# A gated two-branch encoder block: the last two gate tiles of branch B as a pair of seven block products, two more warming products, another seed for near ties

## The chip, the cores and the metric

One core of one Trainium2 chip. The time is device microseconds of one execution of the kernel; the kernel before was run three times (424.71, 424.83 and 425.92 us, median 424.83), and one more execution was profiled.

## The reference

The input is x of 512 tokens by 1024 channels. It is normalised, and one projection gives everything: latents for a dense attention (branch A), queries, keys and values for a sparse attention (branch B), an indexer, a silu gate for each branch, and two sigmoid gates.

```
h = rmsnorm(x, norm_g)
q_lat, c_kv, k_rope, z_a, q_b, k_b, v_b, z_b, q_idx, k_idx, w_idx, gate_a, gate_b = split(h @ w_in)
y_a = mla_attention(...) * silu(z_a)
y_b = dsa_attention(...) * silu(z_b)
merged = sigmoid(gate_a) * (y_a @ w_o_a) + sigmoid(gate_b) * (y_b @ w_o_b)
out = rmsnorm(x + merged @ w_out, final_g)
```

Each gate is 512 tokens by 1024 channels, each silu path 512 by 512.

## The kernel before

The whole program is one function, `tile_block`. It describes the work as some dozens of generators ("threads"), each of which yields steps: an engine, an estimated time, the tiles written and read, and a function that emits the instructions. A planner (`Flow.run`, L192) keeps estimated free times of PE, DVE, ACT, POOL and SP, and emits the step that can start soonest by its estimate. To that start it adds 0.01 times the thread's priority and a `nudge`, a random number below 0.01 us that each thread draws when it is spawned (L154) from a generator seeded with `DRAW` (L151, L258). So the order on every engine is fixed when the program is built, and `DRAW` settles only steps that nearly tie. A step may name two engines (DVE or POOL); the planner takes the one that would end first.

**Precision.** Every fp32 operand of a product is split into a high part (ACT casts it, L314) and a low part (a subtraction on DVE or POOL, L340 or L342), and a product is three matmuls: high by high, high by low, low by high (`mm3`, L417; all matmuls are emitted by `mm`, L407, whose matmul is on L412).

**Projections.** They are computed in tiles of 128 channels by 512 tokens, with the 1024 input channels in 8 blocks. A single tile (`proj`, L959) is 8 x 3 matmuls of 512 columns; its weights come as one load into one of 4 raw buffers and are split in two halves of 512 columns (2 casts, 2 low parts). A pair of tiles (`proj2`, L1009) treats its two weight tiles as four blocks, and the normalised input as four blocks of its own (`input_sums`, L981, whose sums `hs` are already there), and computes the pair by seven block products in place of eight: `prep` makes four sums of weight blocks on DVE or POOL and splits seven blocks; each block product is 4 x 3 matmuls of 256 columns (`times`, L1046); `seven` (L1071) gathers the results with two ACT copies and five DVE sums of 256 columns, while it chains the products on three banks: a bank is added to again only when it has been read. Parts of pairs take at most 10 slots (`PCAP`), parts of other tiles at most 8 (`WCAP`).

**The order of the tiles** is written out in `QUEUE` (L2042). Lower-case names are single tiles and upper-case ones pairs: `ga` and `gb` are the gates of A and B, `za` and `zb` the silu paths, `sb` a key and a query tile of branch B, `VB` its values, and `ou` one preparation of output weights (load, split), which has no product of its own. Loads (`fetcher`, L928), splits (`splitter`, L938) and products (`multiplier`, L951) each go through the list in its order; the preparations of pairs and of output weights run beside the splitter as threads of their own. The products are filling work with low priority between the attention heads, the last of which run from about 300 to 326 us.

**What waits for the tiles.** `y_gate` (L1654) multiplies a branch's attention output by its silu path and, after all pairs are done ("pairs", L1109), splits it for the next product (`s_ys`, the split on L323 and L351). After the last projection of any kind ("projections", L1216) the gates of A, which were sent to DRAM, are loaded back (`fetch_gates`, L1250: eight loads `s_sig<-bias_scratch`). Then `branch_out` (L1713) computes eight tiles of branch A and eight of branch B, each 4 x 3 matmuls of 512 columns on `s_ys,s_w` with weights `w_o`, then the final product with the output weights (`s_wo`), residual and norm.

**The start.** `warm_up` (L517) issues `NWARM` = 14 bf16 matmuls of 256 columns on zeros (L522) while the first loads run; `early_mm` (L686) then has the first products.

Of the kernel before, what the change touches and what calls it, by code (L numbers as in the profile page):

```python
# [19 lines left out]
P = 128  # L20
# [23 lines left out]
class Buf:  # L44


    def __init__(self, tile, name):
        self.tile, self.name, self.w, self.r, self.written = tile, name, 0.0, 0.0, False
        self.by, self.reads = None, {}
# [31 lines left out]
class Step:  # L81
# [7 lines left out]

    def __init__(self, options, outs, ins):  # L90
        self.options, self.outs, self.ins = options, outs, ins


class Get:
# [28 lines left out]
def put(*bufs):  # L123
    for b in bufs:
        b.home.used[b.cls] -= 1
        b.home.free.append(b)
# [7 lines left out]
class Flow:  # L134
# [9 lines left out]
    def __init__(self):  # L144
# [5 lines left out]

        self.draw = random.Random(DRAW)  # L151

# [102 lines left out]
RAW_LAG = {"DVE": 0.125, "POOL": 0.1, "ACT": 0.1}  # L255
BIAS = 0.01
NUDGE = 0.01
DRAW = 53  # L258
PSQUARE = -50
SETTLE = {'PE': {'DVE': 2.0, 'ACT': 2.0, 'POOL': 2.0, 'SP': 1.0}, 'SP': {'DVE': 1.0, 'ACT': 1.0, 'POOL': 1.0}}  # L260
TC_ARGS = {}
# [3 lines left out]
def tile_block(ctx: ExitStack, tc: tile.TileContext, a: dict, out: bass.AP, bias_dram: bass.AP):  # L265
    nc = tc.nc
# [6 lines left out]
    def fixed(name, shape, dt=F32):  # L273
        return Buf(const.tile(shape, dt, name=name), name)
# [24 lines left out]
    def bank(cls):  # L299
        return Get(PS, cls, {"mm": 3, "lg": 2, "pt": 2, "pv": 1, "e": 6}.get(cls))  # L300
# [5 lines left out]
    def bufs(*vs):  # L306
        return [v.buf for v in vs if isinstance(v, View)]
# [94 lines left out]
    def pe(time, outs, ins, emit, count=1):  # L402
        step = Step([("PE", time, emit)], bufs(*outs), bufs(*ins))
        step.count = count
        return step
# [81 lines left out]
    zeros = fixed("zeros", [P, P])  # L487
# [29 lines left out]
    def warm_up():  # L517

        ps = yield bank("pv")
        z = zeros.tile.bitcast(BF16)  # L520
        for _ in range(NWARM):
            yield pe(WARM, [ps.all], [zeros.all], lambda: nc.tensor.matmul(  # L522
                ps.tile[:, :256], z[:, :P], z, start=True, stop=True))
        put(ps)

    def setup_pool():
# [1439 lines left out]
    outs = [(p, c) for p, n in ((1, 2), (7, 4), (2, 2), (6, 2), (5, 4), (4, 2), (3, 2)) for c in range(n)]  # L1966
    for item in QUEUE.split():
        kind, n = item[:2].lower(), item[2:]
# [24 lines left out]
    spawn(setup(), 0)  # L1993
    spawn(loads(), 0)
    spawn(warm_up(), 0)
    spawn(setup_pool(), PSET)
    spawn(early_x(), 0)
# [31 lines left out]
NWARM = 14  # L2029
WARM = 0.22  # L2030
# [8 lines left out]
PHEAD = 4.0  # L2039
OUT_AT = (0, 2, 4, 8, 10, 11, 13)  # L2040
ORDER = [0,1,2,3]
QUEUE = 'ga0 ga1 pe ma0 va0 ga2 za0 ma1 va1 ga3 za1 ma2 ga4 za2 ma3 ga5 za3 sb0 zb0 ga6 ga7 sb1 VB GB0 GB1 sb2 zb1 GB2 GB3 sb3 zb2 GB4 GB5 ou zb3 gb6 ou gb7 ou'  # L2042
LATE = 0.5
SLOW = 1.36
PSUMS = 8.0
# [85 lines left out]
```

## Time and profile before

| | us |
|---|---|
| three runs, median (lowest to highest) | 424.83 (424.71 to 425.92) |
| profiled execution, its own time | 424.27 |
| its span, first to last instruction | 422.5 |
| PE busy | 414.6 |
| DVE busy | 372.9 |
| ACT busy | 265.3 |
| POOL busy | 124.3 |

The profiled execution lasts 1.8 us longer than its span. An engine's busy time is the union of its instructions' times. A matmul is shown with its latency (about 0.39 us for 512 columns), so neighbours overlap, and how long one holds PE is read from start to start. In a timeline, instructions of one kind are merged into one row with their count; the brackets at its end say how long the engine was idle before it and what released it.

### The profile page before, as it was taken

The numbers are of one execution on the slowest core, as the hardware profiler recorded it, in microseconds if no ns is written. First come the engines' busy times: TensorE is split into PE (matmuls) and PEld (weight loads), VectorE is DVE, ScalarE is ACT, GpSimd is POOL, SyncE is SP. The second block draws the span as 40 slices with busy tenths as digits, with TensorE's granted clock in tenths as the row PEclk, the third lists the DMA queues.
The fourth block names the chain that finished last, engine by engine and source line by source line (L and its number), as shares of the span: only waits on it lengthen the run. The fifth ranks groups of instructions, "written<-read, shape, count | busy, mean of one in ns | idle before, by whom it ended". The sixth has DMA issues, their size and how long they took to land.

```text
span 422.5 us, 7070 instructions
## 1 busy us (share of the span) xinstructions
PE 414.6 (98%) x2312; PEld 364.4 (86%) x2312; DVE 372.9 (88%) x797; ACT 265.3 (63%) x596; POOL 124.3 (29%) x139
## 2 busy tenths in 40 slices
PE   8999999999999999999999999999999999999994
PEld 7999878788888888888999988998998888888883
DVE  5689889569999999999999999979799768999985
ACT  6787778576763748635568777694598434336624
POOL 0037768534464659500013000210100000110652
PEclk9999999999999999999999999999999999999998
DMA  7983136746256351454552346245541887248305
GB/s 261 384 303 102 48 97 187 225 119 158 76 154 177 89 158 50 114 150 149 144 169 75 109 142 162 79 149 141 143 151 61 278 310 250 98 145 285 146 1 199
DMA packets 30645, 65.89 MB, mean 156 GB/s; under 512 B 4776, under 2 KB 6200, under 8 KB 30608
## 3 DMA queue, kind: packets, MB, share of 16 engines
q1 hardware_dynamic: 28256, 61.66, 46.3%
q10 hardware_dynamic: 1584, 2.62, 1.7%
q0 software_dynamic: 768, 1.15, 0.9%
q8 instruction: 18, 0.29, 0.3%
q14 instruction: 19, 0.16, 0.1%
HBM read 50.49 MB, written 4.21 MB: 129 GB/s over the span
## 4 chain that ended last, share of the span: by engine, by line
PE 77%; DVE 7%; DMA 6%; ACT 4%; issue 2%; SPq 2%; POOL 0%; POOLq 0%; DVEq 0%; ACTq 0%
PE ps L412 69%; PE ps L429 4%; DMA s_x<-xT 3%; SPq L439 2%; DVE s_tmp L351 2%; DVE s_tmp L340 2%; DMA s_xn<-x 1%; PE ps L1547 1%; PE ps L1548 1%; PE ps L1546 1%; ACT ps L323 1%; DMA raw<-w_ql 1%; DMA s_op<-kpel 1%; ACT junk L323 1%; DVE s_h L340 1%
## 5 line engine op out<-in xcount | busy, mean ns | idle before, releaser
L412 PE MATMUL ps<-s_h,s_w 128*128 128x512 f32 (+1 forms) x732 | 169.9, 379 | 0.0
L412 PEld LDWEIGHTS ps<-s_h,s_w 128*128 128x128 f32 x732 | 128.3, 189 | 22.0
L314 ACT CAST s_w<-raw 128x512 fp32r<-128x512 f32 (+3 forms) x124 | 71.8, 593 | 18.2 <-DMA raw<-w_o 8.4
L342 POOL TENSOR_TENSOR s_w<-raw,s_w 128x512 fp32r<-128x512 f32 (+2 forms) x39 | 48.5, 1253 | 47.6 <-ACT s_w L314 43.7
L340 DVE TENSOR_TENSOR s_w<-raw,s_w 128x512 fp32r<-128x512 f32 (+2 forms) x85 | 55.9, 670 | 4.4 <-ACT s_w L314 3.9
L412 PE MATMUL ps<-s_ys,s_w 128*128 128x512 f32 x192 | 43.8, 389 | 0.0
L412 PEld LDWEIGHTS ps<-s_ys,s_w 128*128 128x128 f32 x192 | 36.0, 188 | 7.5
L323 ACT ACTIVATE s_p<-s_p,sm 128x128 f32<-128x128 f32 (+3 forms) x62 | 32.8, 552 | 4.9 <-DVE sm L1626 4.3
L412 PE MATMUL ps<-s_wo,s_mg 128*128 128x512 f32 (+1 forms) x156 | 33.2, 373 | 0.0
L412 PE MATMUL ps<-s_w,s_xg 128*128 128x328 f32 (+1 forms) x192 | 32.5, 323 | 0.0
L412 PEld LDWEIGHTS ps<-s_wo,s_mg 128*128 128x128 f32 x156 | 27.6, 188 | 5.2
L412 PEld LDWEIGHTS ps<-s_w,s_xg 128*128 128x128 f32 x192 | 31.4, 188 | 0.0
L340 DVE TENSOR_TENSOR s_ph<-ps,s_ph 128x384 fp32r<-128x384 f32 (+1 forms) x48 | 27.6, 592 | 0.7 <-ACT s_ph L314 0.5
L314 ACT CAST s_ph<-ps 128x384 fp32r<-128x384 f32 (+1 forms) x48 | 23.4, 516 | 6.4 <-PE ps L429 5.0
L323 ACT ACTIVATE s_p<-ps,sm 128x128 f32<-128x128 f32 (+3 forms) x32 | 16.8, 528 | 16.7 <-DVE sm L1529 16.6
L342 POOL TENSOR_TENSOR s_p<-s_bias,mask 128x128 f32<-128x128 f32 (+2 forms) x5 | 4.4, 890 | 75.5 <-DMA s_bias<-bias_scratch 75.5
L880 DVE MAX8 sm<-mask 128x8 f32<-128x384 f32 (+2 forms) x48 | 25.7, 548 | 0.2
L881 DVE MATCH_REPLACE8 mask<-sm,mask 128x384 f32<-128x384 f32 (+2 forms) x48 | 25.8, 540 | 0.0
L412 PE MATMUL ps<-s_ph,vv 128*128 128x512 f32 (+3 forms) x128 | 25.1, 318 | 0.0
L429 PE MATMUL ps<-ident,s_p 128*128 128x128 f32 x160 | 23.1, 273 | 0.0
L412 PEld LDWEIGHTS ps<-s_ph,vv 128*128 128x128 f32 x128 | 21.0, 188 | 2.4
L1529 DVE TENSOR_REDUCE sm<-ps 128x1 f32<-128x128 f32 (+3 forms) x32 | 14.8, 480 | 8.2 <-PE ps L1548 7.8
(194 smaller groups left out, 767.6 us busy)
## 6 DMA issues: line engine op xcount, KB each, us to landing
raw<-w_out SPq DMA_DIRECT2D x18, 512.0 KB, 4.8
s_op<-s_op SPq DMA_DIRECT2D x36, 128.0 KB, 2.7
raw<-w_ga SPq DMA_DIRECT2D x8, 512.0 KB, 3.7
raw<-w_gb SPq DMA_DIRECT2D x8, 512.0 KB, 3.6
raw<-w_o SPq DMA_DIRECT2D x16, 256.0 KB, 3.4
s_xn<-x SPq DMA_DIRECT2D x8, 256.0 KB, 5.1
bias_scratch<-s_sig ACTq DMA_DIRECT2D x8, 256.0 KB, 3.7
raw<-w_za SPq DMA_DIRECT2D x4, 512.0 KB
```

What stands on the lines that cost most here:

```text
L314: nc.scalar.copy(dst.ap, src.ap)
L323: nc.scalar.activation(dst.ap, src.ap, func, **kw)
L340: opts.append(("DVE", 0.07 + 0.00104 * x.n, lambda: nc.vector.tensor_tensor(dst.ap, x.ap, y.ap, op=op)))
L342: opts.append(("POOL", 0.15 + 0.0021 * x.n, lambda: nc.gpsimd.tensor_tensor(dst.ap, x.ap, y.ap, op=op)))
L351: lambda: nc.vector.scalar_tensor_tensor(dst.ap, x.ap, sc(s), y.ap, op0=op0, op1=op1))],
L412: nc.tensor.matmul(ps.ap, l.ap, r.ap, start=start and i == 0, stop=stop and i == len(pairs) - 1, skip_group_check=more)
L429: nc.tensor.transpose(d.ap, s.ap, ident.tile)
L439: return Step([("SP", n / 360000.0, lambda: nc.sync.dma_start(d, s))], bufs(dst), bufs(src))
L880: yield Step([("DVE", t, lambda: nc.vector.max(m8.tile, work.tile))], [m8], [work])
L881: yield Step([("DVE", t, lambda: nc.vector.match_replace(work.tile, m8.tile, work.tile, MARK))], [work], [m8])
L1529: yield Step([("DVE", 0.07 + 0.00104 * n, lambda: nc.vector.tensor_reduce(mx.tile[:, 1:2], ps.tile[:, :n], op=ALU.max, axis=AX.X, negate=T ...
L1546: nc.tensor.matmul(o, q0[0:100], k0[0:100], start=True, stop=False)
```

## The change

Gate tiles 6 and 7 of branch B, two single tiles near the end of the list, become a pair directly behind the pair of tiles 4 and 5. The single silu tile `zb3` moves behind it, and of the three preparations of output weights that stood between these tiles, one stays ahead of `zb3` and two come behind it. The last warming step emits three matmuls in place of one, 16 in all, at the same planned time. The seed of the nudges is another.

```diff
+    def then(self, more):
+        (eng, t, emit), = self.options
+        self.options = [(eng, t, lambda: (emit(), more()))]
+        return self
...
-DRAW = 53
+DRAW = 31
...
-        for _ in range(NWARM):
-            yield pe(WARM, [ps.all], [zeros.all], lambda: nc.tensor.matmul(
-                ps.tile[:, :256], z[:, :P], z, start=True, stop=True))
+        def fill(n):
+            return lambda: nc.tensor.matmul(ps.tile[:, :n], z[:, :P], z[:, :n], start=True, stop=True)
+
+        for i in range(NWARM):
+            step = pe(WARM, [ps.all], [zeros.all], fill(256))
+            if i == NWARM - 1:
+                step.then(fill(256)).then(fill(256))
+            yield step
...
-QUEUE = '... GB4 GB5 ou zb3 gb6 ou gb7 ou'
+QUEUE = '... GB4 GB5 GB6 GB7 ou zb3 ou ou'
```

## Rows read from the trace of the kernel before

**Rows 1.** The page: its head, the busy times by engine (busy us, share of the span, instructions), PE's busy and clock lines of the 40 slices, and the shares of the chain that ended last.

```profile
span 422.5 us, 7070 instructions
...
PE 414.6 (98%) x2312; PEld 364.4 (86%) x2312; DVE 372.9 (88%) x797; ACT 265.3 (63%) x596; POOL 124.3 (29%) x139
...
PE   8999999999999999999999999999999999999994
...
PEclk9999999999999999999999999999999999999998
...
PE 77%; DVE 7%; DMA 6%; ACT 4%; issue 2%; SPq 2%; POOL 0%; POOLq 0%; DVEq 0%; ACTq 0%
```

**Rows 2.** Busy time of each engine in seven stretches from 280 to 400 us. Columns: stretch, its length, then for PE, PEld, DVE, ACT and POOL busy us and instructions, then granted TensorE clock, DMA share, GB/s.

```profile
280.00:301.00 21.00, 21.00 (x108) 17.81 (x107) 16.12 (x30) 10.84 (x21) 0.00 (x0) 1.00 0.56 157
301.00:314.00 13.00, 13.00 (x107) 12.83 (x106) 11.74 (x35) 11.74 (x33) 1.77 (x1) 1.00 0.37 122
314.00:326.00 12.00, 12.00 (x65) 10.22 (x64) 12.00 (x22) 11.02 (x22) 0.00 (x0) 1.00 0.23 74
326.00:334.00 8.00, 8.00 (x37) 6.63 (x36) 6.76 (x12) 4.13 (x8) 0.00 (x0) 1.00 0.81 281
334.00:345.00 11.00, 11.00 (x51) 9.09 (x50) 6.08 (x10) 3.56 (x7) 0.00 (x0) 1.00 0.88 314
345.00:360.00 15.00, 15.00 (x68) 12.43 (x67) 12.74 (x21) 6.89 (x12) 0.00 (x0) 1.00 0.75 251
360.00:400.00 40.00, 40.00 (x178) 33.14 (x177) 39.36 (x73) 20.83 (x40) 8.84 (x5) 1.00 0.50 176
```

**Rows 3.** The timeline of PE alone from 334 to 400 us, merged: start, us, engine, line, operation, tiles, shapes, count.

```profile
334.08 40.96 PE L412 MATMUL ps<-s_ys,s_w 128*128 128x512 f32 x180
374.88 3.56 PE L412 MATMUL ps<-s_wo,s_mg 128*128 128x512 f32 x15
```

**Rows 4.** The timeline of PE alone from 301 to 314 us, merged, where the pair of gate tiles 4 and 5 runs.

```profile
301.79 1.60 PE L412 MATMUL ps<-s_hs,s_w 128*128 128x256 f32 x12
303.23 0.62 PE L412 MATMUL ps<-s_op,qhi 128*128 128x128 f32 x4
...
310.06 1.60 PE L412 MATMUL ps<-s_h,s_w 128*128 128x256 f32 x12
311.50 0.81 PE L429 MATMUL ps<-ident,s_p 128*128 128x128 f32 x6
...
313.58 0.60 PE L429 MATMUL ps<-ident,s_p 128*128 128x128 f32 x4
```

**Rows 5.** Groups of DVE's instructions in the stretch from 301 to 334 us: count, busy us, mean ns of one, idle before.

```profile
L340 DVE TENSOR_TENSOR s_w<-raw,s_w 128x512 fp32r<-128x512 f32 x11 | 7.4, 685 | 0.2 <-ACT s_w L314 0.2
L351 DVE SCALAR_TENSOR_TENSOR s_ys<-s_y,s_ys 128x512 fp32r<-128x512 f32 x8 | 5.2, 690 | 0.5 <-ACT s_ys L323 0.5
...
L340 DVE TENSOR_TENSOR s_pair<-ps,s_pair 128x256 f32<-128x256 f32 x5 | 2.1, 417 | 0.0
L340 DVE TENSOR_TENSOR s_wo<-s_wsum,s_wo 128x512 fp32r<-128x512 f32 x3 | 2.1, 685 | 0.7 <-ACT s_wo L314 0.7
L340 DVE TENSOR_TENSOR s_wsum<-raw 128x512 f32<-128x512 f32 x3 | 2.0, 683 | 0.0
L340 DVE TENSOR_TENSOR s_wo<-raw,s_wo 128x512 fp32r<-128x512 f32 x3 | 2.0, 681 | 0.0
```

**Rows 6.** The timeline of DVE alone around 297 us, where the pair of gate tiles 4 and 5 is prepared.

```profile
296.95 0.69 DVE L340 TENSOR_TENSOR s_w<-s_wsum,s_w 128x512 fp32r<-128x512 f32 x1
297.55 0.69 DVE L340 TENSOR_TENSOR s_w<-raw,s_w 128x512 fp32r<-128x512 f32 x1
```

**Rows 7.** Groups of ACT's instructions in the stretch from 301 to 334 us, same columns.

```profile
L314 ACT CAST s_w<-raw 128x512 fp32r<-128x512 f32 x12 | 7.3, 615 | 0.0
...
L323 ACT ACTIVATE s_ys<-s_y 128x512 fp32r<-128x512 f32 x8 | 4.6, 625 | 0.0
...
L314 ACT COPY s_pair<-ps 128x256 f32<-128x256 f32 x2 | 0.7, 362 | 0.3 <-PE ps L412 0.3
```

**Rows 8.** The timeline of SP's queue from 302 to 336 us: start, length of the issues, what is loaded, count.

```profile
302.51 0.33 SPq L439 DMA_DIRECT2D raw<-w_gb  x1
...
313.79 0.34 SPq L439 DMA_DIRECT2D raw<-w_o  x1
...
324.98 0.80 SPq L439 DMA_DIRECT2D raw<-w_o  x2
...
329.53 2.11 SPq L439 DMA_DIRECT2D raw<-w_o  x2
331.69 3.80 SPq L439 DMA_DIRECT2D s_sig<-bias_scratch  x8
```

**Rows 9.** The timeline of ACT alone around 340 us; in square brackets the idle time before and what ended it.

```profile
342.69 0.62 ACT L314 CAST s_w<-raw 128x512 fp32r<-128x512 f32 x1 [7.24 <-DMA raw<-w_o]
```

**Rows 10.** The timeline of all engines at the start of the kernel (0 to 9 us).

```profile
1.05 3.17 PE L522 MATMUL ps<-zeros 128*128 128x256 bf16 x14 [1.05 <-DVE neghalf L473]
...
3.92 1.09 ACT L323 ACTIVATE s_xg<-s_x,normg 128x256 fp32r<-128x256 f32 x3 [0.76 <-DMA normg<-norm_g]
...
4.48 1.96 PE L412 MATMUL ps<-s_xg,s_w 128*128 128x256 f32 x8 [0.26 <-ACT s_xg L323]
...
6.27 1.97 PE L412 MATMUL ps<-s_w,s_xg 128*128 128x328 f32 x12
```

**Rows 11.** Groups of PE's instructions over the whole span, shapes apart.

```profile
L412 PE MATMUL ps<-s_h,s_w 128*128 128x512 f32 x624 | 155.1, 395 | 0.0
...
L412 PE MATMUL ps<-s_hs,s_w 128*128 128x256 f32 x144 | 19.9, 285 | 0.0
...
L412 PE MATMUL ps<-s_h,s_w 128*128 128x256 f32 x108 | 15.0, 283 | 0.0
...
L522 PE MATMUL ps<-zeros 128*128 128x256 bf16 x14 | 3.2, 419 | 1.1 <-DVE neghalf L473 1.1
...
L1547 PE MATMUL ps<-s_op,qhi 96*128 96x128 f32 x8 | 2.2, 281 | 0.4 <-DMA s_op<-kpel 0.4
```

**Rows 12.** The timeline of POOL alone from 250 us on.

```profile
274.45 1.30 POOL L342 TENSOR_TENSOR s_w<-raw,s_w 128x512 fp32r<-128x512 f32 x1 [6.91 <-ACT s_w L314]
304.00 1.77 POOL L342 TENSOR_TENSOR s_wo<-raw,s_wo 128x512 fp32r<-128x512 f32 x1 [28.25 <-ACT s_wo L314]
...
396.06 11.46 POOL L342 TENSOR_TENSOR s_wo<-raw,s_wo 128x512 fp32r<-128x512 f32 x2
```

More of the change, by code (lines that the diff above doesn't have):

```diff
@@ L2041 @@
 ORDER = [0,1,2,3]
-QUEUE = 'ga0 ga1 pe ma0 va0 ga2 za0 ma1 va1 ga3 za1 ma2 ga4 za2 ma3 ga5 za3 sb0 zb0 ga6 ga7 sb1 VB GB0 GB1 sb2 zb1 GB2 GB3 sb3 zb2 GB4 GB5 ou zb3 gb6 ou gb7 ou'
+QUEUE = 'ga0 ga1 pe ma0 va0 ga2 za0 ma1 va1 ga3 za1 ma2 ga4 za2 ma3 ga5 za3 sb0 zb0 ga6 ga7 sb1 VB GB0 GB1 sb2 zb1 GB2 GB3 sb3 zb2 GB4 GB5 GB6 GB7 ou zb3 ou ou'
 LATE = 0.5
```

## The prediction

> **What bounds the kernel now.** I read the page first. The reader is to see two things there: PE is busy in 414.6 of 422.5 us and has 9 in nearly every slice, and the chain that ended last runs through PE for 77% of the span [rows 1]. A busy PE can hide idle time, so I looked for gaps elsewhere. The windows around the change show PE busy for the whole of each, from 280 to 400 us, while DVE goes from 16.1 of 21 us up to all of 12.0 between 314 and 326 us, and POOL does next to nothing [rows 2]. Then the timeline: PE runs 180 products of 512 columns from 334.08 to 374.88 us with no gap [rows 3]. So what a product costs can be read from start to start, and what counts is PE time saved, as long as DVE, ACT and the transfers keep PE supplied.
>
> **The pair on PE.** In 334.08 to 374.88 us, 180 products of 512 columns take 40.80 us, 0.227 each [rows 3]. A block product of a pair is 12 matmuls of 256 columns: 301.79 to 303.23 and 310.06 to 311.50 us are 1.44 us each, 0.120 per matmul [rows 4]. Two single tiles are 2 x 8 x 3 = 48 matmuls of 512 columns: 48 x 0.227 = 10.90 us. A pair is 7 x 4 x 3 = 84 of 256 columns: 84 x 0.120 = 10.08 us. PE saves **0.82 us**. An eighth of the columns goes, but a short matmul carries relatively more fixed time. The Trainium skill, "TensorE: Matmul & The Clock Gate", section "Back-to-back issue gap", gives columns / 2.4 ns plus about 2.5 ns for an isolated matmul. By that estimate the pair would save 48 x 0.2158 - 84 x 0.1092 = 1.19 us, and the rows disagree with it: they show 0.227 and 0.120. I go by the rows.
>
> **The pair on DVE and ACT.** Two single tiles need four low parts on DVE. A pair needs seven low parts, four sums of weight blocks and five 256-column sums of results: seven more instructions of 512 columns at 0.685 us and five at 0.417 [rows 5], 4.80 + 2.09 = 6.9 us busy. Neighbours start 0.60 us apart though each is shown as 0.69 long [rows 6], so the time really taken is nearer 7 x 0.60 + 5 x 0.33 = 5.9 us. ACT gets three more casts at 0.615 and two copies at 0.362, 2.6 us [rows 7]; with 26.9 of 33 us busy from 301 to 334 us [rows 2] it has room. DVE has not: it is busy in 30.5 of those 33 us [rows 2], 2.5 us short of full.
>
> What makes room for 5.9 us? Three preparations of the output weights stand between the last gate tiles now; two move behind zb3, with their instructions on ACT and DVE. Output-weight work on DVE from 301 to 334 us is nine instructions, 2.1 + 2.0 + 2.0 = 6.1 us [rows 5], used only from 374.88 us on [rows 3]. Of the eight low parts of the gated values, 5.2 us [rows 5], half belong to branch B and are wanted only after branch A's eight tiles. Behind 334 us DVE has 4.9 us idle up to 345 and 2.3 us up to 360 [rows 2]. So 5.9 us has 2.5 + 7.2 = 9.7 us to go into if the order lets it. I cost it at nothing; its cover is this deferrable work. If the cover is gone, PE stalls for up to 5.9 - 2.5 = 3.4 us. From both sides, then: 0 to +3.4 us. I take 0, since the nearest row, the pair before this one (301.79 to 313.58 us), shows PE without a gap while DVE is 90% busy [rows 2, 4].
>
> **What moves with it.** The split of gated values waits until all pairs are done: now at 313.58 us, with three tiles of PE work after it [rows 4]. Afterwards only zb3 is behind the last pair, 24 x 0.227 = 5.4 us. The four parts of branch A need 4 x 0.625 us on ACT and 4 x 0.69 on DVE, which overlap [rows 5, 7]; they fit, with about 2 us over. If they are late, the first output tile of branch A is late by the same. Silu tile zb3 now comes last; its result is wanted by branch B only, which costs nothing while A's tiles, 8 x 12 x 0.227 = 21.8 us, cover it.
>
> On SP's queue the order of loads changes: both gate tiles, one output-weight load and zb3, and then two output-weight loads ahead of the first tile of branch A's weights. Each issue takes 0.33 us of the queue [rows 8], so the issues cost nothing beside PE. What can be late is behind them: before the burst of eight gate loads at 331.69 us, five loads of branch weights have been issued (313.79, two at 324.98, two at 329.53) [rows 8], and the next weights to be cast make ACT wait 7.24 us, until 342.69 [rows 9]. Five tiles at 12 x 0.227 = 2.72 us keep PE supplied from 334.08 to 347.7 us, and the sixth is split by about 344.1 (a cast of 0.62 and a low part of 0.69 behind 342.69), so there are 3.6 us of slack. One tile fewer costs nothing; two fewer would cost 5.4 - 3.6 = 1.8 us. Bounds 0 to +1.8; I take 0, since the raw buffers of the pair come free well before zb3 ends.
>
> **Two warming products.** The fourteen now issued start at 1.05 us and last 3.17; the first real product starts at 4.48, released by ACT, after 0.26 us of PE idle [rows 10]. Fourteen in 3.17 us with the last one's pipeline in it are about 0.21 us each, which is 256 columns at 1.2 GHz, though the page's clock line has 9 from its first slice [rows 1]. Two more are 0.43 us, against 0.26 us idle plus about 0.2 us of the last one's own latency (it is shown as 0.42 long [rows 11]): they end about when ACT releases the real work. Cost between 0 and 0.17 us. A gain is possible if the clock rises sooner: the eight products from 4.48 take 1.79 us until the next group starts at 6.27 [rows 10]; at 0.12 to 0.17 each they would take 1.2 us, so at most 0.6 us. The idle before them is also a wait on data that stays. I take 0, with -0.6 to +0.2 as ends.
>
> **The draw.** It changes tiny priorities, so instructions that tie may swap everywhere. PE's visible idle time is small: 0.4 us at one wait for a DMA [rows 11] besides the start. It can win about 0.5 us, and by the same measure lose as much or, where a swap makes an operand late, more. I take 0, with -0.5 to +0.8.
>
> **Sum.** -0.82 + 0 + 0 + 0 + 0 = -0.8 us against the profiled 424.27: 423.45. The median of the runs shown, 424.83, stands 0.56 above the profiled execution, so I forecast **424.0 us**. No change means within 0.3%, 1.27 us, about what a measurement can tell: 423.56 to 426.10. The forecast lies inside it, though on the faster side.
>
> **Rivals.**
> *Faster by more (423.2 us).* The start gains and ties fall well: -0.82 - 0.4 at the start - 0.4 from ties. For it: PE bounds the whole span, so whatever PE gains early arrives at the end. Against it: the rows show little idle time to win. It is decided by 0.45 us beyond the pair's saving.
>
> *Slower (427.4 us): DVE late for the last pair.* The place is 301 to 334 us. If the preparations are ordered so that nothing deferrable moves behind 334 us, DVE's 5.9 us meets 2.5 us of room, PE stalls 3.4 us and the net is +2.6 us. For it: DVE is full from 314 to 326 us already, and POOL, free there, is weak help: a low part took it 1.30 us at 274.45 and 1.77 at 304.00, but two took 11.46 us from 396.06, beside a full DVE [rows 2, 12]. The Trainium skill, "SBUF — State Buffer", section "SBUF: two separate sides", says that the port pair that the two share is an exclusive lock, held for the whole instruction; by that rule POOL gives no relief here, and the trace agrees as far as those 11.46 us go. Against it: 6.1 us of output-weight work can move, and two thirds of it is moved behind zb3 by the change. It decides against the change where less than 1.3 us of it leaves the stretch (3.4 - 1.3 = 2.1 us of stall, 0.82 back).
>
> *Nothing gained (424.8 us).* A stall of some 0.8 us, at the pair's own sums or at the split of gated values, takes PE's saving back.
>
> **How the numbers follow.** Forecast case 0.36, its own range 423.5 to 424.9. Nothing gained 0.10. Faster by more 0.34: the bounds at the start and of the ties together (-1.1) make it common enough. Slower 0.20. So faster by over 0.3% has 0.34, within 0.3% 0.46, slower 0.20. The range runs from 422.6 (most of both small gains) to 426.4 (a net of +1.6, nearly half of the DVE stall or most of the late-weights one), which leaves out about 2 in 10.
>
> **What would show it.** Right: 192 matmuls of 256 columns on `s_hs,s_w` and 144 on `s_h,s_w` in place of 144 and 108, 576 of 512 columns in place of 624 [rows 11], no PE gap from 300 to 345 us, the first branch-A product (`s_ys`) starting about 0.8 us earlier than 334.08, output-weight work after 334 us, and the same tail. The DVE rival would show as PE idle in front of a block product, released by DVE's low part of `s_w`, between 313 and 334 us. Late weights would show as PE waiting on a cast that waits on `w_o`. A start that gains shows as the product group of 6.27 us starting earlier. The forecast is wrong if `s_ys` starts 0.8 us earlier and the end does not, or if it starts later than now.

## The result: slower by 5.6 us, and the profile after

The changed kernel takes **430.40 us** (430.28 to 430.56, four runs) against 424.77 of the kernel before beside it: ratio 1.0131, 95% interval 1.0115 to 1.0148. The forecast was 424.0 with a range from 422.6 to 426.4, a little faster than before but within what counted as no change. The result is slower, and outside that range. The profiled span grew from 422.50 to 428.61 us.

First the page of the changed kernel, to be held against [rows 1].

```profile
span 428.6 us, 7194 instructions
...
PE 415.5 (97%) x2350; PEld 365.7 (85%) x2350; DVE 386.0 (90%) x806; ACT 265.8 (62%) x597; POOL 126.7 (30%) x146
...
PE   9999999899999999999999999999999999999992
...
PE 51%; DVE 27%; DMA 9%; ACT 6%; issue 4%; SPq 1%; POOL 0%; POOLq 0%; ACTq 0%; DVEq 0%
```

PE is as busy as before; the busy time that was added stands on DVE (13 us, in part longer instructions and not more work, as shown below), whose share of the chain that ended last went from 7 to 27%. PE's line has an 8 in the eighth slice, some 75 us in: far ahead of the gate tiles that the change is about. And it ends in 2 where before it ended in 4.

PE's groups over the span, shapes apart: the products are those that were forecast, 192 and 144 short ones and 576 long ones in place of those in [rows 11].

```profile
L418 PE MATMUL ps<-s_h,s_w 128*128 128x512 f32 x576 | 144.0, 396 | 0.0
L418 PE MATMUL ps<-s_hs,s_w 128*128 128x256 f32 x192 | 26.3, 285 | 0.8 <-DVE s_pair L346 0.8
L418 PE MATMUL ps<-s_h,s_w 128*128 128x256 f32 x144 | 20.4, 286 | 0.3 <-ACT s_pair L320 0.3
L528 PE MATMUL ps<-zeros 128*128 128x256 bf16 x16 | 3.6, 416 | 1.1 <-DVE neghalf L479 1.1
```

PE's waits from 8 to 420 us (what was waited for, us in total, times, longest). The kernel before had one such wait in this stretch, 0.4 us for a DMA [rows 11].

```profile
PE ps L870 <- DVE mask L357: 1.5, 1, 1.5
PE ps L418 <- DVE mask L357: 0.8, 1, 0.8
PE ps L418 <- DVE s_pair L346: 0.8, 1, 0.8
PE ps L418 <- DVE s_xr L357: 0.5, 1, 0.5
PE ps L418 <- ACT s_pair L320: 0.3, 1, 0.3
```

All five are for work of DVE, or of ACT behind it. To see what each is worth I cut the span at three events that every kernel has: **A** ends at the first product of gate tiles 4 and 5 (301.79 us in [rows 4]), **B** at the first `s_ys` product (334.08 in [rows 3]), **C** at the start of the last matmul, **D** is the tail.

| kernel | A | B | C | D | span |
|---|---|---|---|---|---|
| before | 301.79 | 32.29 | 81.89 | 6.53 | 422.50 |
| after | 305.30 | 32.38 | 82.65 | 8.28 | 428.61 |
| difference | +3.51 | +0.09 | +0.76 | +1.75 | +6.11 |

The pair lies in B, and there nothing is lost. More than half of the loss lies in A, where the computation is unchanged but for the two warming products and only the order can differ; most of the rest is in the tail. From start to start of the products, the three waits in A (0.84, 1.51 and 0.26 us) cost 3.2 of its 3.51 us.

**Stretch A.** DVE alone from 64 to 80 us, after:

```profile
66.22 0.67 DVE L346 TENSOR_TENSOR s_tmp<-ps,ropec 128x512 f32<-128x512 f32 x1
66.80 2.27 DVE L346 TENSOR_TENSOR s_tmp<-s_tmp,ropes 128x512 f32<-128x512 f32 x1
68.99 0.74 DVE L357 SCALAR_TENSOR_TENSOR mask<-ps,widx,mask 128x512 f32<-128x512 f32 x1
...
76.55 2.36 DVE L357 SCALAR_TENSOR_TENSOR s_qpe<-s_tmp,s_qpe 128x512 fp32r<-128x512 f32 x2
78.84 1.00 DVE L357 SCALAR_TENSOR_TENSOR mask<-ps,widx,mask 128x384 f32<-128x384 f32 x2
```

POOL in the same stretch, after:

```profile
65.39 1.28 POOL L348 TENSOR_TENSOR s_w<-raw,s_w 128x512 fp32r<-128x512 f32 x1 [2.59 <-ACT s_w L320]
...
67.21 1.30 POOL L348 TENSOR_TENSOR s_w<-raw,s_w 128x512 fp32r<-128x512 f32 x1
...
76.98 1.39 POOL L348 TENSOR_TENSOR s_w<-raw,s_w 128x512 fp32r<-128x512 f32 x1 [2.16 <-issue]
```

And PE, after:

```profile
69.78 1.67 PE L418 MATMUL ps<-s_lat,s_w 128*128 128x512 f32 x6 [0.84 <-DVE mask L357]
...
79.50 0.50 PE L870 MATMUL ps<-s_qs,s_qs 96*128 96x512 f32 x1 [1.51 <-DVE mask L357]
```

The multiplication by `ropes` from 66.80 takes DVE 2.27 us instead of some 0.6: it ends at 69.07, 0.56 us behind POOL's instruction (67.21 + 1.30 = 68.51). The two `s_qpe` end at 78.91, 0.54 us behind POOL's 78.37. The `mask` sum queued behind each is what PE waits for. In the kernel before POOL itself does that multiplication, twice, beside the same work:

```profile
65.35 1.29 POOL L342 TENSOR_TENSOR s_tmp<-s_tmp,ropes 128x512 f32<-128x512 f32 x1
...
67.86 1.29 POOL L342 TENSOR_TENSOR s_tmp<-s_tmp,ropes 128x512 f32<-128x512 f32 x1
```

So ahead of each wait stands an instruction that the new order has put on DVE, or on a place in its queue, where it meets POOL; in the kernel before the two `s_qpe` take 1.28 us together. That these two swaps alone make the waits was not tried by itself. **Stretch B**, PE alone after:

```profile
328.62 1.28 PE L418 MATMUL ps<-s_h,s_w 128*128 128x256 f32 x9
330.68 1.69 PE L418 MATMUL ps<-s_hs,s_w 128*128 128x256 f32 x12 [0.78 <-DVE s_pair L346]
332.21 5.63 PE L418 MATMUL ps<-s_h,s_w 128*128 128x512 f32 x24
337.68 7.64 PE L418 MATMUL ps<-s_ys,s_w 128*128 128x512 f32 x33
```

One wait at the pair's last block product, released by DVE's sum of results. Branch A then starts without a gap.

**Tail.** DVE alone from 405 us on, after: the low part of an output weight takes 1.78 us, and the last sums over partial products come at 410.03 us. In the kernel before they stand at 402.66, so they come 7.4 us later, of which branch A's later start explains 3.6 (337.68 against 334.08).

```profile
405.93 1.78 DVE L346 TENSOR_TENSOR s_wo<-s_wsum,s_wo 128x512 fp32r<-128x512 f32 x1
407.63 1.27 DVE L357 SCALAR_TENSOR_TENSOR s_part<-ps,s_part 128x512 f32<-128x512 f32 x2
...
410.03 3.69 DVE L346 TENSOR_TENSOR s_xr<-s_xr,s_part 128x512 f32<-128x512 f32 x6
```

The same sums in the kernel before:

```profile
402.66 3.70 DVE L340 TENSOR_TENSOR s_xr<-s_xr,s_part 128x512 f32<-128x512 f32 x6
```

### The profile page after: what moved, and what is told of

Its sections match the earlier page's. It is cut to its first block, busy times and chain, and to the rows that moved or that the text cites. A ratio compares the mean times of both kernels' runs of the same rounds, so it can differ in the third digit from the quotient of the medians.

```text
span 428.6 us, 7194 instructions
## 1 busy us (share of the span) xinstructions
PE 415.5 (97%) x2350; PEld 365.7 (85%) x2350; DVE 386.0 (90%) x806; ACT 265.8 (62%) x597; POOL 126.7 (30%) x146
## 4 chain that ended last, share of the span: by engine, by line
PE 51%; DVE 27%; DMA 9%; ACT 6%; issue 4%; SPq 1%; POOL 0%; POOLq 0%; ACTq 0%; DVEq 0%
PE ps L418 44%; PE ps L435 4%; DMA raw<-w_out 3%; DVE s_pair L346 3%; DVE s_wo L346 3%; DMA s_x<-xT 3%; DVE s_tmp L346 2%; DVE s_w L346 2%; DVE s_mg L346 2%; DVE s_tmp L357 2%; DVE s_wsum L346 2%; DMA raw<-w_ql 1%; DMA raw<-w_o 1%; ACT s_w L320 1%; PE ps L1559 1%
## 5 line engine op out<-in xcount | busy, mean ns | idle before, releaser
L418 PE MATMUL ps<-s_h,s_w 128*128 128x512 f32 (+1 forms) x720 | 164.2, 374 | 0.3 <-ACT s_pair L320 0.3
L418 PEld LDWEIGHTS ps<-s_h,s_w 128*128 128x128 f32 x720 | 123.8, 189 | 20.3 <-ACT s_pair L320 0.5
L348 POOL TENSOR_TENSOR s_w<-raw,s_w 128x512 fp32r<-128x512 f32 (+2 forms) x42 | 54.6, 1306 | 72.2 <-ACT s_w L320 54.4
L346 DVE TENSOR_TENSOR s_w<-raw,s_w 128x512 fp32r<-128x512 f32 (+3 forms) x84 | 53.8, 654 | 3.8 <-ACT s_w L320 3.3
L329 ACT ACTIVATE s_p<-s_p,sm 128x256 f32<-128x256 f32 (+3 forms) x56 | 29.4, 545 | 6.8 <-DVE sm L1638 6.7
L418 PEld LDWEIGHTS ps<-s_w,s_xg 128*128 128x128 f32 x192 | 31.4, 188 | 0.1
L418 PE MATMUL ps<-s_hs,s_w 128*128 128x256 f32 x192 | 26.3, 285 | 0.8 <-DVE s_pair L346 0.8
L418 PEld LDWEIGHTS ps<-s_hs,s_w 128*128 128x128 f32 x192 | 24.5, 191 | 1.2 <-DVE s_pair L346 1.0
```

The costliest lines, as they stand in the source:

```text
L329: nc.scalar.activation(dst.ap, src.ap, func, **kw)
L346: opts.append(("DVE", 0.07 + 0.00104 * x.n, lambda: nc.vector.tensor_tensor(dst.ap, x.ap, y.ap, op=op)))
L348: opts.append(("POOL", 0.15 + 0.0021 * x.n, lambda: nc.gpsimd.tensor_tensor(dst.ap, x.ap, y.ap, op=op)))
L418: nc.tensor.matmul(ps.ap, l.ap, r.ap, start=start and i == 0, stop=stop and i == len(pairs) - 1, skip_group_check=more)
```

## The experiments

Times are medians; the kernel before took 424.9 to 425.3 us beside them. A ratio is to the kernel before, run beside it.

### The parts of the change, one at a time

```
e1  -DRAW = 53                               +DRAW = 31
e2  -... GB4 GB5 ou zb3 gb6 ou gb7 ou        +... GB4 GB5 GB6 GB7 ou zb3 ou ou
e3  +if i == NWARM - 1: step.then(fill(256)).then(fill(256))
e4  e2 and e3 together, DRAW = 53            e8  the same, DRAW = 2
```

**e1**, the draw alone.

> The kernel before with the seed 31 in place of 53 and nothing else. If the seed's order makes the loss (PE is already 3.1 us late near 100 us in the changed kernel, long before the last pair), this is slower by 3 us or more: 428 to 433. If the pair makes it, this stays within 1.3 us of the kernel before (424 to 426).

Measured 438.92 us, ratio 1.0308 [1.0268, 1.0349]. **e2**, the new `QUEUE` alone (seed 53, fourteen warming products).

> The kernel before with the list of tiles of the changed one (pair of gate tiles 6 and 7, seed 53, fourteen warming products). If the seed makes the loss and the pair is worth what PE saves: 423.7 to 424.3, 0.8 us below the kernel before. If DVE is late for the last pair, as in the rival with 427.4: 426 to 428, with PE idle before a block product near 325 us.

Measured 430.61 us, ratio 1.0106 [1.0074, 1.0139]. **e3**, the two warming products alone.

> The kernel before with sixteen warming products. In the changed kernel the first real product started 0.12 us later and the next group 0.23 us later, and the clock rose no sooner: so 0.1 to 0.3 us slower here (424.9 to 425.1). If the warming products raise the clock sooner: 424.2 to 424.6.

Measured 424.81 us, ratio 0.9987 [0.9968, 1.0006]. **e4**, pair and warming products, `DRAW = 53`.

> The changed kernel with the seed put back to 53. If the seed makes the loss: about 6 us faster than the changed kernel, 423.8 to 424.5. If the pair makes it: 429 to 431.

Measured 429.48 us, ratio 1.0086 [1.0057, 1.0115]. **e8**, the changed kernel with `DRAW = 2`.

> The changed kernel with the seed 2. Its order by the planner ends within 0.1 us of the seeds 53 and 31. If seeds that the planner holds equal are equal on the chip, 429 to 431; if the end stall near 410 us depends on the order, anywhere from 424 to 436.

Measured 430.07 us, ratio 1.0123 [1.0101, 1.0145].

The warming products do nothing to the median. They may narrow the spread: 7 of the 18 executions of the kernel before that ran beside e3 took 426.4 to 427.2 us, and none of e3's ten took over 425.44. The profiled execution of e2 (431.26 us) shows how such a time can come about: its first twelve products of 328 columns take 3.04 us, against 1.80 in the trace of the kernel before, and it reaches the end of A 2.1 us later. Whether two more warming products prevent that was not tried by itself.

The draw by itself costs 14 us and the pair by itself some 5, and together they cost 5.6: the parts do not add. PE of e1 near its end, and two windows of it (columns as in [rows 2]):

```profile
414.20 10.04 PE L412 MATMUL ps<-s_wo,s_mg 128*128 128x512 f32 x41 [6.47 <-DVE s_wo L340]
```

```profile
405.00:411.00 6.00, 2.73 (x18) 2.24 (x16) 6.00 (x9) 0.46 (x1) 1.44 (x1) 1.00 0.00 0
411.00:418.00 7.00, 3.80 (x13) 3.32 (x14) 3.14 (x6) 0.00 (x0) 0.00 (x0) 0.51 0.01 4
```

PE waits 6.47 us for a low part of an output weight from DVE, and the granted clock falls to the lower of its two levels, 1.2 GHz (0.51), around it. The two `mask` waits near 70 and 79 us are in e1 as well (0.59 and 1.52 us), and with draw 2 with and without the pair (e8 and, further down, e10): they belong to the draw, not to the pair.

### Where the pair loses with draw 53

In the cut of the table above, e4 against e3 (the same without the pair) is A 301.90 against 302.34, **B 31.41 against 32.29**, **C 87.30 against 81.89**, D 6.44 against 6.52. PE's saving of 0.88 us is there, and 5.4 us are lost behind the start of branch A. SP's queue, ACT and PE of e4:

```profile
303.81 0.33 SPq L445 DMA_DIRECT2D raw<-w_zb  x1
321.68 0.99 SPq L445 DMA_DIRECT2D raw<-w_out  x2
323.13 0.33 SPq L445 DMA_DIRECT2D raw<-w_o  x1
...
328.21 0.80 SPq L445 DMA_DIRECT2D raw<-w_o  x2
329.75 0.38 SPq L445 DMA_DIRECT2D raw<-w_out  x1
330.18 4.60 SPq L445 DMA_DIRECT2D s_sig<-bias_scratch  x8
335.17 0.98 SPq L445 DMA_DIRECT2D raw<-w_o  x2
```

```profile
341.45 0.62 ACT L320 CAST s_w<-raw 128x512 fp32r<-128x512 f32 x1 [3.85 <-DMA raw<-w_o]
...
410.04 0.63 ACT L329 ACTIVATE junk<-s_xr 128x512 f32<-128x512 f32 x1 [9.50 <-DVE s_xr L357]
...
411.21 0.60 ACT L320 CAST s_wo<-s_wsum 128x512 fp32r<-128x512 f32 x1
```

```profile
333.31 8.32 PE L418 MATMUL ps<-s_ys,s_w 128*128 128x512 f32 x36
342.12 8.05 PE L418 MATMUL ps<-s_ys,s_w 128*128 128x512 f32 x33 [0.49 <-ACT s_w L320]
...
411.87 3.22 PE L418 MATMUL ps<-s_wo,s_mg 128*128 128x512 f32 x6 [1.94 <-ACT s_wo L320]
```

Two places. (1) Only three loads of branch weights are issued before the burst of eight, where there were five [rows 8]. Three tiles, 36 products, last PE until 341.6; the next cast stands at 341.45. Behind the load of zb3's weights SP's queue waits 17.5 us for a raw buffer, until 321.68: the pair holds its buffers up to its last two low parts, on DVE from 320.98. The kernel before issues branch weights from 313.79 on [rows 8]. The seven splits of gated values, now one block on DVE, hold up little: the first load behind the burst is issued at 335.17, within 0.4 us of the end of the burst's issues (330.18 + 4.60 = 334.78).

```profile
320.98 1.27 DVE L346 TENSOR_TENSOR s_w<-raw,s_w 128x512 fp32r<-128x512 f32 x2
...
329.04 0.68 DVE L346 TENSOR_TENSOR s_w<-raw,s_w 128x512 fp32r<-128x512 f32 x1
329.64 4.29 DVE L357 SCALAR_TENSOR_TENSOR s_ys<-s_y,s_ys 128x512 fp32r<-128x512 f32 x7
```

(2) At the end ACT's last cast of an output weight is queued behind squares that wait 9.50 us for DVE; PE idles 1.94 us for it, and then runs at the lower clock, as a window of e4 shows:

```profile
411.90:415.40 3.50, 3.50 (x8) 2.45 (x9) 1.94 (x4) 1.10 (x4) 0.00 (x0) 0.51 0.00 0
```

Four experiments on this. **e5**: e4 without the seven low parts of the last pair, order unchanged. The kernel leaves out the low part of these two gate tiles, and the products read the high part in its place; of the edit:

```
step = soon(lo_part(lo.all, x, hi.all))
if first[:2] == ("w_gb", 6): step.options = [(e, t, lambda: None) for e, t, _ in step.options]
```

> The pair and sixteen warming products with seed 53, in the same order of all instructions as in the kernel without the new seed; only the seven low parts of the last pair's weight blocks are not issued (products use the high part in their place, so the low part of these two gate tiles is left out), six of them on DVE. PE's work is the same. If the pair's loss is DVE time that lands at the end of the kernel, 6 x 0.60 = 3.6 us of it go and with them PE's wait of 2.3 us near 410 us: 424 to 425.5. If the order itself is the cause, 428.5 to 430 as without this edit.

Measured 428.58 us, ratio 1.0082 [1.0057, 1.0107]: 0.9 us less than e4, but by the ratios (1.0086 for e4) the two cannot be told apart. **e6**: e3 (no pair) with the low parts of three late silu and gate tiles and of one product's output weights computed twice, `step.options = [(e, t, lambda: (emit(), emit())) ...]`, ten instructions more on DVE and POOL.

> The kernel before with sixteen warming products, in the same order; the six low parts of zb3, gb6 and gb7 and the four of the first output weights are computed twice, ten more DVE or POOL instructions (about 6 us) from 304 to 326 us, no pair. If DVE time added in this stretch comes out at the end: 427.5 to 431. If the slack of DVE between 334 and 360 us takes it up, as the prediction had it: 424.6 to 425.6.

Measured 431.91 us, ratio 1.0158 [1.0137, 1.0179]. **e7**: e4 with POOL's three output-weight instructions at 395 to 402 us given to DVE (`yield on_dve(...)` for `yield soon(...)`).

> The pair and sixteen warming products with seed 53 in the same order; the three instructions of the output weights that POOL has near 395 to 402 us are issued on DVE at their place. If what hurts there is DVE and POOL keeping each other from the operands (three DVE instructions took 3.80 us beside POOL): 426.5 to 428.5. If it is the amount of work on DVE alone: 1.8 us more of it, 430 to 432.

Measured 428.57 us, ratio 1.009 [1.0054, 1.0126]. **e9**: e4 with `PSQUARE = 0` for -50, which puts the last cast ahead of the squares.

> The pair with 16 warming products and draw 53 (the kernel that took 429.48 us), with the constant PSQUARE raised from -50 to 0, so that the order written out lets ScalarE's last output-weight cast go ahead of the squares that wait for VectorE's sums; nothing is computed otherwise. Theory A (the end of the kernel is lost because that cast stands in ScalarE's queue behind squares that wait for VectorE): TensorE's 1.94 us wait for s_wo at 411.9 us and the half clock of 3.4 us behind it (about 1.7 us) go, the last product starts near 417 to 418 us and the time is 426 to 427.5 us; the stall at 342 us stays. Theory B (VectorE is simply out of time from 380 us on, and whatever is moved, its end comes as late): 428.5 to 430 us.

Measured 429.38 us, ratio 1.0098 [1.0078, 1.0118].

e6 says that added low parts are dear: ten of them cost 7.1 us beside e3, in an order made without them. Some 1.7 us of that, by estimate, is the clock, which is at its lower level (0.50) from 353.5 to 356.8 us, behind a wait of 1.67 us for branch weights (3.4 us at half speed do 1.7 us of work).

e5 by its time alone seems to say the opposite, but its trace shows that the loss has moved. At the end the wait of 1.94 us shrinks to waits of 0.48 and 0.22, and the clock stays up. At 344.25 us the wait for branch weights grows from 0.49 to 1.75 us, and there the clock falls, as a window of e5 shows:

```profile
345.20:348.50 3.30, 3.30 (x9) 2.53 (x9) 3.22 (x6) 1.79 (x4) 0.00 (x0) 0.50 0.55 164
```

So without the pair's own low parts the end is shorter, and what that gives goes again at the branch weights. e7 splits the 1.94 us at the end into waits of 0.59, 0.34 and 0.44 us and keeps the clock up, and is no faster than e4 by its ratio, since 1.59 us are lost at 344.15. And e9 speaks against ACT's queue as the whole of the loss at the end. In it the cast goes early and the wait at 411 us is gone, yet another stands 10 us earlier:

```profile
402.23 12.52 PE L418 MATMUL ps<-s_wo,s_mg 128*128 128x512 f32 x65 [1.61 <-DVE s_wo L346]
```

and the tail is 7.85 us for 6.44; the wait for branch weights is 1.34 us. Mending one wait moved the loss along the order. That left two theories: the pair itself costs 4 to 5 us, or the order drawn for the rest does.

### The same draw with and without the pair

**e10** and **e11** are e3 with `DRAW = 2` and `DRAW = 1`; **e12** is e4 with `DRAW = 1`.

> The kernel before with 16 warming products and draw 2, without the pair; beside it stands the pair with draw 2, 430.07 us. Theory A (the pair by itself costs some 4 to 5 us through VectorE and the late weights, whatever the draw): 425 to 426 us. Theory B (each draw is an order of its own, whose stalls have little to do with the pair): anywhere between 425 and 439 us, as draw 31 had 438.9 without and 430.4 with the pair; 428 to 436 us speaks for it.

> The kernel before with 16 warming products and draw 1, without the pair. Theory A (draw 53 is an ordinary draw, and the pair is what costs): 424 to 427 us. Theory B (draw 53 without the pair is an unusually good order, and an ordinary draw has stalls of some us more): 428 to 436 us.

> The pair with 16 warming products and draw 1. Theory A (the pair costs 4 to 5 us beside the same draw without it): 4 to 5 us above the run of draw 1 without the pair. Theory B (draws differ by more than the pair is worth; the pair's saving of 0.8 us on TensorE stands and the stalls are the draw's): 428 to 432 us, and not above the run without the pair by more than 1 us.

| draw | without the pair | with the pair |
|---|---|---|
| 53 | 424.81 (e3) | 429.48 (e4) |
| 31 | 438.92 (e1) | 430.40 (after) |
| 2 | 429.91 (e10) | 430.07 (e8) |
| 1 | 431.17 (e11) | 429.02 (e12) |

e1 has fourteen warming products and its partner sixteen; e3 shows that this does not move the median.

Beside the same draw the pair makes +4.7, -8.5, +0.2 and -2.1 us. The first theory, a fixed cost of 4 to 5 us, is refuted. Without the pair, draw 53 is 5 us better than the next of these.

### Only the order behind 310 us drawn anew

The draw is kept at 53 up to 310 us of the planned time and taken from a second seed after that, so that the order in A stays as in the kernel before:

```
t = Thread(gen, prio, (self.draw if self.free["PE"] < SINCE else self.later).random() * NUDGE)
DRAW, SINCE, LATER = 53, 310, 1        # e14: 6, e17: 7 with the pair; e15: 2, e16: 6, e18: 3 without
```

> The pair with 16 warming products and draw 53 (429.48 us), with the near ties drawn anew only for threads that start after the planner's 310 us (seed 1 from there on), so everything up to there is the same. Theory A (the pair's own low parts and its late output weights cost the branch weights and the end some 4 to 5 us, in whatever order the rest stands): 428.5 to 431 us, with TensorE's wait for branch weights near 342 us and one of 1.5 us or more for s_wo near 400 to 412 us. Theory B (the saving of 0.8 us on TensorE stands, and whether those two waits arise is a matter of the order drawn for the work behind it): the three orders of this kind spread by 2 us or more, and one of them comes below 426 us.

> As the run before it with seed 6 from 310 us on. Theory A: 428.5 to 431 us with both waits. Theory B: anywhere between 423.5 and 431 us.

> The kernel before with 16 warming products (424.81 us), without the pair, the near ties drawn anew after 310 us with seed 2; the planner's own end for it is the same as without the redraw. Theory A (without the pair the low parts find their room): 424.3 to 426 us. Theory B (draw 53 of the kernel before is an order picked among many, and another one of the same planned length has waits at the end too): 427 to 431 us.

> As the run before it with seed 6 from 310 us on. Theory A: 424.3 to 426 us. Theory B: 427 to 431 us.

> The pair redrawn after 310 us with seed 7, as in the two runs with seeds 1 (424.83 us) and 6 (428.40 us). If the pair saves 0.8 us on TensorE and draws decide the rest, then from the middle of the gates to the start of branch A it takes 31.4 us as in the other pairs (32.3 us without), TensorE waits 0.4 to 1.7 us for branch weights near 342 us, which no kernel without the pair does, and the time is anywhere from 424 to 429 us.

> Without the pair, redrawn after 310 us with seed 3, as in the two runs with seeds 2 (427.05 us) and 6 (425.15 us): 32.3 us from the middle of the gates to the start of branch A, no wait near 342 us, and the time between 424.5 and 429 us by the waits for output weights from 395 us on.

The column "342 us" sums what PE's products lose from start to start (beyond 0.227 us each) between 338 and 352 us. A, B, C and D are of one profiled execution each; A differs by up to 0.9 us between these, though its order is the same.

| kernel | us | ratio to before | A | B | C | D | 342 us |
|---|---|---|---|---|---|---|---|
| pair: e4 | 429.48 | 1.0086 | 301.90 | 31.41 | 87.30 | 6.44 | 1.03 |
| pair: e13 | 424.83 | 0.9984 [0.9969, 1.0000] | 302.48 | 31.42 | 82.69 | 6.52 | 0.78 |
| pair: e14 | 428.40 | 1.0071 [1.0047, 1.0094] | 301.94 | 31.41 | 85.77 | 7.61 | 1.70 |
| pair: e17 | 427.18 | 1.0046 [1.0031, 1.0062] | 302.16 | 31.41 | 83.28 | 8.21 | 1.38 |
| no pair: e3 | 424.81 | 0.9987 | 302.34 | 32.29 | 81.89 | 6.52 | 0 |
| no pair: e15 | 427.05 | 1.0041 [1.0022, 1.0061] | 302.67 | 32.28 | 83.64 | 6.52 | 0 |
| no pair: e16 | 425.15 | 0.9997 [0.9981, 1.0013] | 302.60 | 32.31 | 81.89 | 6.64 | 0 |
| no pair: e18 | 425.70 | 0.9994 [0.9973, 1.0015] | 302.78 | 32.31 | 82.40 | 6.66 | 0 |

This settles three things. B is 31.4 us with the pair and 32.3 without, whatever the order: **PE saves 0.88 us**. The wait for branch weights near 342 us comes with the pair whenever this draw leads up to it (0.8 to 1.7 us here) and in none of this table's kernels without it, so in these kernels the pair's gain is paid back by late weights. And what C and D hold beside that, 0 to 4.3 us, differs with the order alone: it is nearly nothing in e13 and 4.3 in e4 with the same pair, nothing in e3 and 1.7 in e15 without it.

The late weights can be followed further in the traces. All eleven kernels with the pair issue two or three loads of branch weights ahead of the burst, all those without it five or six. In seven with the pair and draw 53 up to there (e2, e4, e7, e9, e13, e14, e17) the burst's issues end 1.3 to 2.9 us behind the first product of branch A, and the column "342 us" is 0.8 to 2.1. In e5 they end 2.4 us behind it, and the lower clock adds to the loss. In the changed kernel, e8 and e12 they end 0.6 to 1.8 us ahead of that product, and 0 to 0.25 us are lost. No run moves the burst by itself, so this is seen side by side and not shown as the cause.

In e13 PE has no gap from 391.82 us to the end, with ACT's last cast ahead of the squares:

```profile
391.82 19.41 PE L418 MATMUL ps<-s_wo,s_mg 128*128 128x512 f32 x96
411.07 5.80 PE L418 MATMUL ps<-s_wo,qhi 128*128 128x512 f32 x36
```

```profile
399.95 0.62 ACT L320 CAST s_wo<-raw 128x512 fp32r<-128x512 f32 x1
407.04 0.42 ACT L329 ACTIVATE junk<-s_xr 128x256 f32<-128x256 f32 x1 [6.47 <-DVE s_xr L357]
```

e13 is the fastest kernel with the pair, well ahead of the changed one, and cannot be told from the kernel before. What stays open: whether over many orders the pair wins or loses. The answer changes sign from draw to draw, and no mean (the last table: 427.5 with, 425.7 without; the four draws: 429.7 and 431.2) rests on enough orders. Nor was an order tried that has the pair and draw 53 up to 310 us without the late weights.

## Why the prediction was wrong

- **The pair on PE: right.** Forecast 0.82 us, measured 0.88: B is 31.39 to 31.42 us in ten of the kernels with the pair (all but the changed one with its 0.78 us wait) and 32.28 to 32.38 in the kernels without it, apart from e6 with its doubled low parts.
- **The pair on DVE, "I cost it at nothing": half right.** From 314 to 334 us the cover held: with draw 53 no block product waits, and in the changed kernel one does, 0.78 us, released by a sum of results. DVE's busy time in 334 to 345 us went from 6.08 [rows 2] to 10.20 (and it is 10.20 too in the first 11 us of branch A there, from 337.68), as foreseen. The slow rival's place was right for that one wait; its price of 3.4 us was not.
- **The split of gated values, "they fit": right.** Branch A starts straight behind zb3 in all kernels with the pair, and in e4 the split, seven in a block of 4.29 us, delays the next load by 0.4 us at most.
- **Late loads, "Bounds 0 to +1.8; I take 0": the wrong end.** The reason given was that "the raw buffers of the pair come free well before zb3 ends". They do: at 321.68 us in e4, where branch A starts at 333.31. But by then the kernel before has long begun with its branch weights (313.79 [rows 8]). So three loads instead of five stand ahead of the burst, just the case priced at 1.8, and 0.8 to 1.7 us were lost in the four kernels of the last table. In the changed kernel itself branch A starts late enough (337.68) for its weights, and this wait is absent.
- **Two warming products, 0: right for the median.** e3 shows -0.13% with an interval across zero; what they do to the spread is open.
- **The draw, "I take 0, with -0.5 to +0.8": the step that failed.** In the changed kernel stretch A, which the pair does not touch, alone is 3.51 us longer, and the first `s_ys` product starts at 337.68 us, where a start 0.8 us ahead of 334.08 was forecast. By itself the draw measures some +14 us (e1), beside the pair +0.9 (after against e4); draws 2 and 1 stand 5.1 and 6.4 us above draw 53 without the pair. The argument took the 0.4 us of idle time in the kernel before as a measure of both sides, and no row stands behind the +0.8. The idle time measures what can be won. What can be lost depends on how little slack the order leaves, and [rows 2] had shown that: DVE at 39.36 of 40 us behind 360 us.
- **"The same tail", with no term in the sum: the second step that failed.** In the changed kernel the tail took 1.75 us more, and C 0.76. With the draw left at 53 (e4) the waits at 342 and 412 us and the lower clock cost enough for 429.48 us, which lies outside the range as well; with another order behind 310 us (e13) the same pair shows little of that. DVE is full to the end, so what is added or swapped there comes out as later sums.
- **The premise under the sum** was that the order stays and only the listed parts move. The order is planned anew as a whole, from changed costs and another seed; terms taken from the old order's slack then say little about the new one.

The rival that came nearest, "DVE late for the last pair" at 427.4 us, had the right engine, and the wrong place for most of the loss.

## What to carry to other kernels

Where an order is planned as a whole, a seed or a queue entry is not a small edit: run the old computation under several seeds before putting a price on a new one, and compare new and old under the same seeds, since one pair of runs here says anything from -8.5 to +4.7 us. Idle time of the bounding engine bounds what a reordering can win; what it can lose is read from the slack of the engine that feeds it. And where work is moved, ask not only when its result is wanted but how long its inputs hold their buffers, and which loads wait for those.

## What the runs showed of the hardware

- **Two engines on one port.** Beside POOL, an instruction of DVE that reads only SBUF ran until POOL's was over plus 0.55 us (2.27 us for one and 2.36 for two, above), while one that reads PSUM kept its 0.67 us beside POOL's from 65.39 us. The Trainium skill, "SBUF — State Buffer", section "SBUF: two separate sides", says that whichever of a DVE instruction with two SBUF inputs and a GpSimd instruction starts first has the shared pair for the whole instruction and that the other fully blocks. The second case agrees: POOL's record starts at 76.98 us, that of the `s_qpe` that is held up at 77.15. In the first case DVE waits in the same way, but its record starts at 66.80, ahead of POOL's 67.21, so the recorded starts do not show there who came first.
- **A wait can cost twice.** Behind 1.94 us of idle PE in e4 the granted clock was 0.51 over the window of 3.5 us shown above, which by estimate costs some 1.7 us more; in e1 it was 0.51 from 411 to 418 us around a wait of 6.47. It happens in the middle too: 0.50 behind a wait of 1.75 us at 344 us in e5, and 0.50 behind one of 1.67 us at 352 us in e6. Behind a wait of 1.71 us in e14 and of 1.61 in e9 it stayed at 1.00, so the length of the wait alone does not tell these apart. Seven of the twenty profiled kernels have such a stretch ahead of their last products (e1, e2, e4, e5, e6, e11, e12), and in them it is part of what one order costs more than another.
